# The second product of an MLP by Strassen sets, summed in DRAM

## The chip, the cores and the metric

One core of a Trainium2 chip runs the kernel. The metric is the device time of one execution in microseconds (us); for the kernel before, the median of three runs.

## What is computed

One decoder block in fp32: two gated mixers, a projection back to the residual (W_out), and an MLP with a squared ReLU (first product W1, second product W2), each behind an RMS norm. Cut to what matters here:

```python
def rmsnorm(x, g):
    return x * lax.rsqrt(jnp.mean(x * x, axis=-1, keepdims=True) + NORM_EPS) * g

def reference(x, meta_tokens, ...):                      # SEQ 512, D_MODEL 2048, D_FF 8192, 16 meta tokens
    h = concatenate([meta, x])
    u = rmsnorm(h, norm1_g)
    ...                                                  # two gated mixers, merged
    h = h + merged @ w_out
    u2 = rmsnorm(h, norm2_g)
    h = h + jnp.square(jax.nn.relu(u2 @ mlp_w1)) @ mlp_w2
    return rmsnorm(h, final_g)[:, N_META:]
```

## The kernel before

Activations lie with channels on partitions and the 512 real tokens along the free axis. Every fp32 product is made of three fp32r products: weights and activations are split into a high and a low part, and `mm3` (L609) issues high x high, high x low, low x high into one PSUM bank. A weight chunk is 128x1024 (512 KB). The class `Weights` (L34) loads it on SP's queue into a ring of four raw buffers (L78), ACT writes its high part (L102), DVE its low part (L103), into rings of four. Loads run ahead as raw buffers come free, splits two products ahead of their use.

**Stages.** The mixers and W_out run until about 1209 us. Behind the last W_out tiles (`job_WO`, L521) the residual is stored to DRAM (`h_sp`, eight pieces of 512 KB, two output tiles each), and `pre_scale` and `forms` (L546, L570) prepare W1's operands: the sums and differences of the residual that a Strassen product needs, split into high and low parts (`X`).

**W1** (L633 to L664) runs j over 32 pairs of inner tiles. Each j is one Strassen set: seven products of 8 x 3 = 24 matmuls with 256 columns each, into three banks A, B and C. The four weight blocks a, b, c, d of the set give seven weights; DVE forms four sums of them (L92) in place or in extra buffers. Results are put together from the banks with three helpers, p1, u2 and q5 (copies by ACT, sums by DVE: L641, L650, L653), scaled and clamped on DVE, squared on ACT (L662), and stored as `y_sp[j]` on POOL's queue (L663).

**W2** (L680 to L708) is a plain product: seven groups of eight inner tiles and one of four, and for each group 16 output tiles. A group's y tiles are loaded from `y_sp` on ACT's queue (L684, `yl`), split by ACT (L687, `fh`) and DVE (L688, `fl`); an output tile takes 24 matmuls of 512 columns, and DVE adds it to the accumulator `acc` (L708), which was loaded from `h_sp` at W2's start.

**The tail** (L738 to L773) does the last four inner tiles in two halves of 256 tokens, with weights kept in `keep`, and the final norm and the stores.

A scheduler sets the order of instructions on each engine from the order of the code and from the pools; within an engine they run in that order.

Of the kernel before, what the change touches and what calls it, by code (L numbers as in the profile page):

```python
# [16 lines left out]
P = 128  # L17
# [10 lines left out]
CH = 1024  # L28

# [4 lines left out]
class Weights:  # L34
# [34 lines left out]
    @staticmethod  # L69
    def _cuts(i):  # L70

        return [slice(0, CH // 2), slice(CH // 2, CH)] if i == 0 else [slice(0, CH)]

    def _load(self):
        i = self.loaded
        t = self.pool.tile([P, CH], F32, tag="raw", name=f"raw{i}", bufs=self.raw_bufs)
        for s in self._cuts(i):
            self.nc.sync.dma_start(t[:, s], self.loads[i][:, s])  # L78
        self.raw[i] = t
        self.loaded += 1  # L80
        self.live += 1

    def _split(self):
# [3 lines left out]
        for o, x, y in sums:  # L87
            if o not in self.raw:
                self.raw[o] = self.sums.tile([P, CH], F32, tag="sum", name=f"sum{o[1]}{o[0]}", bufs=3)
            while max(k for k in (x, y) if isinstance(k, int)) >= self.loaded:  # L90
                self._load()
            nc.vector.tensor_tensor(self.raw[o], self.raw[x], self.raw[y], op=ALU.add)  # L92
        while isinstance(key, int) and key >= self.loaded:
            self._load()
        raw = self.raw[key]
        if i in self.place:
            hi, lo = self.place[i]
        else:
# [15 lines left out]
    def ready(self, splits):  # L114
        while self.split < min(splits, len(self.ops)):
# [14 lines left out]
def build(ctx, tc, nc, xt_d, par_d, w_in_d, gate_d, pool_d, w_out_d, w1_d, w2_d, w2t_d, out_d):  # L130
# [46 lines left out]
    F_TILES = [8] * 7 + [4, 4]  # L177
    for f, n in enumerate(F_TILES):
        srcs = [w2_d[f * KD + m] for m in range(KD)] if n == 8 else [
            w2t_d[(f - 7) * 8 + m] for m in range(8)]  # L180
        for s in srcs:
            W.chunk(s)
# [58 lines left out]
    y_sp = [dram.tile([P, 2 * SEQ], F32, name=f"ysp{j}") for j in range(32)]  # L241
# [38 lines left out]
    with ExitStack() as mx:  # L280
# [289 lines left out]
        def pre_scale():  # L570
# [4 lines left out]
            V.tensor_scalar(s, t, 2.0 / D, EPS, op0=ALU.mult, op1=ALU.add)  # L575
# [19 lines left out]
    side.close()  # L595
    ep = xa.enter_context(tc.tile_pool(name="ep", bufs=1, side="right", reuse_waits="tile"))
    W.sums = ep
# [16 lines left out]
    if True:  # L614

        def part(name, j):
            return ep.tile([P, HS], F32, tag=name, name=f"{name}_{j}", bufs=2)

        def bank(name, j):
            return ps.tile([P, 512], F32, tag="ps", name=f"ps_{name}{j}")[:, :HS]  # L620

        def product(o, r, first):
            hi, lo = W.next()
            xh, xl = X[r]
            for k in range(8):
                s, c = slice(k * P, (k + 1) * P), slice(k * HS, (k + 1) * HS)
                mm3(o, (hi[:, s], lo[:, s]), xh[:, c], xl[:, c], first and k == 0, k == 7)
# [5 lines left out]
        for j in range(32):  # L633
            A, B, C = (bank(x, j) for x in "ABC")
            p1, u2, q5 = (part(x, j) for x in ("p1", "u2", "q5"))
            y = ep.tile([P, 2 * SEQ], F32, tag="y", name=f"y{j}", bufs=2)
            product(A, "x11", True)
            S.activation(p1, A, AF.Copy)
            W.advance()
            product(C, "x21", True)  # L640
            V.tensor_tensor(y[:, :HS], C, p1, op=ALU.add)  # L641
            W.advance()
            product(A, "t2", False)
            S.activation(u2, A, AF.Copy)
            W.advance()
            product(B, "t1", True)
            S.activation(q5, B, AF.Copy)
            W.advance()
            product(A, "t3", False)
            V.tensor_tensor(y[:, 3 * HS :], A, q5, op=ALU.add)  # L650
            W.advance()
            product(B, "x22", False)
            V.tensor_tensor(y[:, HS : 2 * HS], B, u2, op=ALU.add)  # L653
            W.advance()
            product(A, "t4", False)

            V.scalar_tensor_tensor(y[:, :SEQ], y[:, :SEQ], 0.0, rho, op0=ALU.max, op1=ALU.mult)
            V.scalar_tensor_tensor(y[:, 3 * HS :], y[:, 3 * HS :], 0.0, rho[:, HS:], op0=ALU.min,
                                   op1=ALU.mult)
            V.scalar_tensor_tensor(y[:, SEQ : 3 * HS], A, 0.0, rho[:, :HS], op0=ALU.min,  # L660
                                   op1=ALU.mult)
            S.activation(y, y, AF.Square)  # L662
            nc.gpsimd.dma_start(y_sp[j], y)  # L663
            W.advance()  # L664
    xa.close()

# [4 lines left out]


    n = len(W.ops)
    keep = [fp.tile([P, 8 * CH], F32R, name=f"keep{x}") for x in "hl"]
    for j in range(8):
        s = slice(j * CH, (j + 1) * CH)
        W.place[n - 8 + j] = (keep[0][:, s], keep[1][:, s])
    ht = fp.tile([P, KD, SEQ], F32, name="acc")
    first = 0
    for f, n in enumerate(F_TILES):  # L680
        fs = []
        for m in range(first, first + n):
            y = ftmp(f"yl{m}")
            nc.scalar.dma_start(y, y_sp[m // 2][:, (m % 2) * SEQ : (m % 2 + 1) * SEQ])  # L684
            fh = fp.tile([P, SEQ], F32R, tag="fh", name=f"fh{m}", bufs=11)
            fl = fp.tile([P, SEQ], F32R, tag="fl", name=f"fl{m}", bufs=11)
            S.activation(fh, y, AF.Copy)  # L687
            V.tensor_tensor(fl, y, fh.bitcast(F32), op=ALU.subtract)  # L688
            fs.append((fh, fl))
        if f == 0:  # L690
            for k in range(8):
                nc.scalar.dma_start(ht.rearrange("p (a k) t -> p a k t", a=2)[:, :, k, :],
                                    h_sp[k].rearrange("p (a s) -> p a s", a=2))
        first += n
        if f == len(F_TILES) - 1:
            break
        for m in range(KD):
            if n == 8 or m % 2 == 0:
                hi, lo = W.next()
            at = 0 if n == 8 else (m % 2) * n * P  # L700
            t = ps.tile([P, 512], F32, tag="ps", name=f"ps_w2_{f}_{m}")
# [107 lines left out]
```

## Time and profile before

| what | us |
|---|---|
| median of 3 runs | 2622.49 (2621.5 to 2624.58) |
| the profiled execution | 2616.56 |
| its span (first to last instruction) | 2614.8 |
| TensorE (PE) busy | 2550.6, 98% |
| VectorE (DVE) busy | 1498.0, 57% |
| ScalarE (ACT) busy | 896.7, 34% |
| GpSimd (POOL) busy | 182.9, 7% |

Busy times are of the whole span. Stages have different limits, so what counts for a stage is read in windows of it, and in what TensorE waits for there. A matmul's duration in a timeline overlaps the next one's; the distance between the starts of two is what it costs. Weight loads into TensorE (PEld) overlap matmuls.

### The profile page before, as it was taken

What the parts mean: (1) busy time and instruction counts of PE and PEld (TensorE: products, weight loads), DVE (VectorE), ACT (ScalarE), POOL (GpSimd) and SP (SyncE); (2) the same over time, 40 slices, a digit from 0 to 9 for tenths busy, and PEclk for the clock granted to TensorE, in tenths of its full rate; (3) what the DMA queues carried; (4) which work ended last, traced back from release to release, by engine and by line L of the source; (5) the groups of instructions that cost most, each with busy time, mean ns of one, the idle gap of its engine ahead of it and who ended that gap; (6) DMA issues with size and microseconds to landing.
All of it is one profiled execution on the core that took longest, in us unless ns stands there. A gap on an engine that the chain in (4) does not pass through costs nothing.

```text
span 2614.8 us, 36302 instructions
## 1 busy us (share of the span) xinstructions
PE 2550.6 (98%) x15380; PEld 2280.4 (87%) x15380; DVE 1498.0 (57%) x1759; ACT 896.7 (34%) x1096; POOL 182.9 (7%) x154
## 2 busy tenths in 40 slices
PE   8999999999999999995999999999999999999997
PEld 7888898989888898974999999999978888888887
DVE  8834574445733574449877777777644434443456
ACT  5522242223322242234444444444422222222234
POOL 2100011100211011312000000000000000000000
PEclk9999999999999999997999999999999999999999
DMA  5332223222322223231433343333463323332331
GB/s 189 97 97 89 97 73 110 93 92 86 100 94 95 91 81 105 95 119 45 134 135 127 121 138 133 133 124 121 160 215 129 129 97 129 129 129 97 125 113 65
DMA packets 91075, 296.19 MB, mean 113 GB/s; under 512 B 9760, under 2 KB 13984, under 8 KB 90912
## 3 DMA queue, kind: packets, MB, share of 16 engines
q1 hardware_dynamic: 73616, 251.82, 29.1%
q10 hardware_dynamic: 11536, 21.07, 2.4%
q0 software_dynamic: 5760, 20.97, 2.1%
q8 instruction: 120, 1.97, 0.3%
q14 instruction: 43, 0.35, 0.0%
HBM read 268.66 MB, written 25.17 MB: 112 GB/s over the span
## 4 chain that ended last, share of the span: by engine, by line
PE 91%; DVE 4%; DMA 2%; issue 1%; ACT 1%; POOL 0%; SPq 0%; ACTq 0%; DVEq 0%
PE ps_w L612 25%; PE ps_A L612 13%; PE ps_vp L332 7%; PE ps_gl L332 7%; PE ps_vl L332 7%; PE ps_gp L332 6%; PE ps_ge L332 6%; PE ps_wo L332 6%; PE ps_B L612 5%; PE ps_C L612 3%; PE ps_w2l L612 2%; PE ps_pw L332 2%; PE ga L332 2%; DMA raw<-w 1%; DVE wlo L103 1%
## 5 line engine op out<-in xcount | busy, mean ns | idle before, releaser
L102 ACT ACTIVATE whi<-raw 128x1024 fp32r<-128x1024 f32 (+1 forms) x489 | 517.6, 1059 | 1293.6 <-PE ps_w L612 434.0
L103 DVE TENSOR_TENSOR wlo<-raw,whi 128x1024 fp32r<-128x1024 f32 (+1 forms) x489 | 614.0, 1257 | 289.5 <-ACT whi L102 284.3
L612 PE MATMUL ps_w<-fh,whi 128*128 128x512 f32 x960 | 374.1, 390 | 6.6 <-ACT fh L687 6.6
L612 PE MATMUL ps_w<-fl,whi 128*128 128x512 f32 x960 | 374.1, 390 | 0.4 <-DVE fl L688 0.4
L612 PE MATMUL ps_w<-fh,wlo 128*128 128x512 f32 x960 | 373.5, 390 | 0.0
L708 DVE TENSOR_TENSOR acc<-ps_w,acc 128x512 f32<-128x512 f32 x128 | 88.5, 691 | 353.6 <-PE ps_w L612 353.6
L612 PEld LDWEIGHTS ps_w<-fh,whi 128*128 128x128 f32 x960 | 180.5, 188 | 44.9 <-ACT fh L687 7.3
L612 PEld LDWEIGHTS ps_w<-fl,whi 128*128 128x128 f32 x960 | 180.6, 188 | 39.0 <-DVE fl L688 1.5
L612 PEld LDWEIGHTS ps_w<-fh,wlo 128*128 128x128 f32 x960 | 180.6, 188 | 37.4
L332 PE MATMUL ps_vl<-uh,whi 128*128 128x264 f32 x512 | 106.0, 289 | 7.4 <-ACT whi L102 7.0
L332 PE MATMUL ps_vl<-uh,wlo 128*128 128x264 f32 x512 | 105.3, 287 | 0.0
L332 PE MATMUL ps_vl<-ul,whi 128*128 128x264 f32 x512 | 105.2, 287 | 0.0
L332 PE MATMUL ps_vp<-ul,whi 128*128 128x264 f32 x512 | 104.4, 285 | 0.0
L332 PE MATMUL ps_vp<-uh,wlo 128*128 128x264 f32 x512 | 104.3, 285 | 0.0
L332 PE MATMUL ps_vp<-uh,whi 128*128 128x264 f32 x512 | 104.2, 285 | 0.0
L332 PE MATMUL ps_gl<-ul,whi 128*128 128x512 f32 x256 | 101.2, 395 | 0.0
L332 PE MATMUL ps_gp<-ul,whi 128*128 128x512 f32 x256 | 101.2, 395 | 0.0
L332 PE MATMUL ps_ge<-ul,whi 128*128 128x512 f32 x256 | 101.2, 395 | 0.0
L332 PE MATMUL ps_gp<-uh,whi 128*128 128x512 f32 x256 | 100.7, 393 | 0.0
L332 PE MATMUL ps_ge<-uh,wlo 128*128 128x512 f32 x256 | 100.7, 393 | 0.0
L332 PE MATMUL ps_gl<-uh,wlo 128*128 128x512 f32 x256 | 100.7, 393 | 0.0
L332 PE MATMUL ps_gp<-uh,wlo 128*128 128x512 f32 x256 | 100.6, 393 | 0.0
(758 smaller groups left out, 6021.3 us busy)
## 6 DMA issues: line engine op xcount, KB each, us to landing
raw<-w SPq DMA_DIRECT2D x240, 512.0 KB, 3.6
raw<-w_in SPq DMA_DIRECT2D x159, 512.0 KB, 3.7
raw<-w_out SPq DMA_DIRECT2D x32, 512.0 KB, 3.2
ysp<-y POOLq DMA_DIRECT2D x32, 512.0 KB, 3.0
yl<-ysp ACTq DMA_DIRECT2D x64, 256.0 KB, 4.3
raw<-w2t SPq DMA_DIRECT2D x16, 512.0 KB, 3.3
ht<-xt SPq DMA_DIRECT2D x16, 264.0 KB, 6.6
raw<-gate SPq DMA_DIRECT2D x8, 512.0 KB, 3.2
```

Of the source, the lines that this page charges most:

```text
L102: nc.scalar.activation(hi[:, s], raw[:, s], AF.Copy)
L103: nc.vector.tensor_tensor(lo[:, s], raw[:, s], hi[:, s].bitcast(F32), op=ALU.subtract)
L332: PE.matmul(o, a, r, start=first and i == 0, stop=last and i == 2)
L612: PE.matmul(o, a, b, start=first and i == 0, stop=last and i == 2, skip_group_check=True)
L708: V.tensor_tensor(h, t, h, op=ALU.add)
```

## The change

W2's first 60 inner tiles (`JS` = 30 pairs) become Strassen sets as in W1. 37 steps t = 1 to 37 run; step t has the outputs p = t mod 8 (four tiles: an output pair for two halves) and sums over up to eight pairs of inner tiles, the last eight written before t. So each pair is used in eight steps in a row, the window moves on by one pair a step, and the first and last seven steps hold 1 to 7 pairs. A product of n pairs has 3n matmuls of 256 columns; its weights are n x 128 wide. A pair lies in one of nine slots (`slot`, seven forms of 256 tokens, high and low, 7 KB each on a partition), loaded on POOL's queue, split into high parts by ACT (L729) and low parts by DVE (L730). The seven forms are made in W1, where DVE computes four more (L705 to L708) into `t`; a pair is stored in two pieces. A step's result e (four quarters: DVE L742 and L746, ACT L744) is added to `h_sp` in DRAM by a DMA on POOL's queue with an accumulating write (L752). The tail's y tiles and the accumulator are loaded on POOL's queue behind the steps. In W_out, `pre_scale` stands behind the second pair of tiles, not the fourth, and one set of forms follows every second pair. The class `Weights` learns widths under 1024 and a limit for its look-ahead; the permutation `ORDER` of output channels goes along.

```diff
-    if True:
+    def strassen(name, pool, operand, put):
...
+        product(A, "x11", True)
+        S.activation(p1, A, AF.Copy)
+        W.advance()
+        product(C, "x21", True)
+        put("11", C, p1)
+        W.advance()
...
+        product(A, "t3", False)
+        put("22", A, q5)
+        W.advance()
+        product(B, "x22", False)
+        put("12", B, u2)
+        W.advance()
+        product(A, "t4", False)
+        put("21", A, None)
+        W.advance()
...
+        nc.gpsimd.dma_start(y_sp[j][:, 4 * HS :], y[:, : 3 * HS])
...
+        V.tensor_tensor(t1, x11, x12, op=ALU.subtract)
+        V.tensor_tensor(t3, x22, x12, op=ALU.subtract)
+        V.scalar_tensor_tensor(t2, x22, -1.0, t1, op0=ALU.mult, op1=ALU.subtract)
+        V.scalar_tensor_tensor(t4, t2, -1.0, x21, op0=ALU.mult, op1=ALU.subtract)
+        nc.gpsimd.dma_start(y_sp[j][:, : 4 * HS], tt)
...
+        def load_slot(j):
+            if j < JS:
+                slots[j] = sl.tile([P, 2, 7 * HS], F32R, tag="slot", name=f"slot{j}", bufs=WIN + 1)
+                nc.gpsimd.dma_start(slots[j][:, 1].bitcast(F32), y_sp[j])
+
+        def split_slot(j):
+            if j < JS:
+                hi, lo = slots[j][:, 0], slots[j][:, 1]
+                S.activation(hi, lo.bitcast(F32), AF.Copy)
+                V.tensor_tensor(lo, lo.bitcast(F32), hi.bitcast(F32), op=ALU.subtract)
+
+        for j in range(3):
+            load_slot(j)
+        split_slot(0)
+        for t, p, js in steps:
+            e = eb.tile([P, 2 * SEQ], F32, tag="e", name=f"e{t}", bufs=2)
...
+                if c == "11":
+                    split_slot(t)
+
+            strassen(f"b{t}", eb, lambda r: [tuple(slots[j][:, i, at(r)] for i in range(2)) for j in js],
+                     put)
+            nc.gpsimd.dma_start(h_sp[p], e, accum_op=ALU.add)
+            load_slot(t + 2)
...
-                    if mp_ == 3:
+                    if mp_ == 1:
                         pre_scale()
-                        forms(0)
-                        forms(2)
-                    elif mp_ > 3 and mp_ % 2 == 1:
+                    if mp_ % 2 == 1:
                         forms(mp_ - 1)
...
-            nc.scalar.dma_start(y, y_sp[m // 2][:, (m % 2) * SEQ : (m % 2 + 1) * SEQ])
...
+        nc.gpsimd.dma_start(y, y_sp[m // 2][:, c])
...
+        nc.gpsimd.dma_start(ht[:, 2 * q : 2 * q + 2, :].rearrange("p a s -> p (a s)"), h_sp[ORDER[q]])
```

The order of instructions moves at three places. The first is POOL's queue from W1's end on. Before, it ends with W1's stores; nothing else follows until the program ends:

```order
L663 DMA ysp28_134<-y28_16085 128x1024
L663 DMA ysp29_135<-y29_16313 128x1024
L663 DMA ysp30_136<-y30_16541 128x1024
L663 DMA ysp31_137<-y31_16769 128x1024
L804 UNCONDITIONAL_BRANCH
```

In the changed kernel slot loads and accumulating stores follow (names: `hsp` is the residual in DRAM, `ysp` the stored forms, `e` a step's result):

```order
L699 DMA ysp30_136<-y30_16720 128x1024
L699 DMA ysp31_137<-y31_16948 128x1024
L724 DMA slot0_17187<-ysp0_106 128x1792
L724 DMA slot1_17189<-ysp1_107 128x1792
L724 DMA slot2_17191<-ysp2_108 128x1792
L724 DMA slot3_17275<-ysp3_109 128x1792
L724 DMA slot4_17378<-ysp4_110 128x1792
L724 DMA slot5_17502<-ysp5_111 128x1792
L752 DMA hsp1_99<-e1_17195 128x1024
L724 DMA slot6_17647<-ysp6_112 128x1792
L724 DMA slot7_17813<-ysp7_113 128x1792
L724 DMA slot8_18000<-ysp8_114 128x1792
L752 DMA hsp2_100<-e2_17277 128x1024
```

The first six slot loads stand behind y31's store; those of slots 6 to 8 stand behind the first step's accumulating store.

The second place is DVE in the changed kernel's second step, which has no counterpart before (`wlo441` to `wlo445` are low parts of step 2's weights, `wlo446` is of step 3, `e2` is step 2's result, and L730 splits slots):

```order
L100 TENSOR_TENSOR raw341_17235<-raw341_17235,sum340s2_17293 128x256
L742 TENSOR_TENSOR e2_17277<-ps_Cb2_17280,p1_b2_17281 128x256
L730 TENSOR_TENSOR slot3_17275<-slot3_17275 128x1792
L112 TENSOR_TENSOR wlo441_17296<-sum340s2_17293,whi441_17295 128x256
L112 TENSOR_TENSOR wlo442_17309<-sum340s1_17291,whi442_17308 128x256
L112 TENSOR_TENSOR wlo443_17321<-raw342_17246,whi443_17320 128x256
L112 TENSOR_TENSOR wlo444_17337<-raw341_17235,whi444_17336 128x256
L730 TENSOR_TENSOR slot4_17378<-slot4_17378 128x1792
L746 SCALAR_TENSOR_TENSOR e2_17277<-ps_Ab2_17278,q5_b2_17283 128x256
L112 TENSOR_TENSOR wlo445_17350<-raw343_17256,whi445_17349 128x256
L742 TENSOR_TENSOR e2_17277<-ps_Bb2_17279,u2_b2_17282 128x256
L112 TENSOR_TENSOR wlo446_17363<-raw344_17324,whi446_17362 128x384
```

Slots 3 and 4 are split inside step 2, whose matmuls read slots 0 and 1; the last of the nine, slot 8, is split in step 3.

The third place is DVE in one full Strassen set. Before, in W1 (`wlo353` to `wlo356` and the sums are of the set's and the next set's weights, the y lines are puts):

```order
L92 TENSOR_TENSOR raw289_14128<-raw289_14128,sum288s2_14289 128x1024
L103 TENSOR_TENSOR wlo352_14351<-raw290_14160,whi352_14350 128x1024
L641 TENSOR_TENSOR y20_14261<-ps_C20_14257,p1_20_14258 128x256
L103 TENSOR_TENSOR wlo353_14385<-raw289_14128,whi353_14384 128x1024
L103 TENSOR_TENSOR wlo354_14416<-raw291_14191,whi354_14415 128x1024
L103 TENSOR_TENSOR wlo355_14447<-raw292_14354,whi355_14446 128x1024
L92 TENSOR_TENSOR sum292s1_14515<-raw294_14388,raw295_14419 128x1024
L650 TENSOR_TENSOR y20_14261<-ps_A20_14255,q5_20_14260 128x256
L103 TENSOR_TENSOR wlo356_14480<-raw293_14356,whi356_14479 128x1024
```

In the changed kernel, W1's set j = 19, with the forms of j = 18 ahead:

```order
L112 TENSOR_TENSOR wlo343_14183<-sum284s2_14180,whi343_14182 128x1024
L112 TENSOR_TENSOR wlo344_14212<-sum284s1_14178,whi344_14211 128x1024
L705 TENSOR_TENSOR t18_14140<-y18_13912 128x256
L706 TENSOR_TENSOR t18_14140<-y18_13912 128x256
L707 SCALAR_TENSOR_TENSOR t18_14140<-y18_13912,t18_14140 128x256
L112 TENSOR_TENSOR wlo345_14242<-raw286_14045,whi345_14241 128x1024
L708 SCALAR_TENSOR_TENSOR t18_14140<-t18_14140,y18_13912 128x256
L100 TENSOR_TENSOR raw285_14013<-raw285_14013,sum284s2_14180 128x1024
L686 TENSOR_TENSOR y19_14146<-ps_C19_14149,p1_19_14150 128x256
L112 TENSOR_TENSOR wlo346_14276<-raw285_14013,whi346_14275 128x1024
L112 TENSOR_TENSOR wlo347_14308<-raw287_14077,whi347_14307 128x1024
L112 TENSOR_TENSOR wlo348_14340<-raw288_14245,whi348_14339 128x1024
```

and W2's step 19, the same stretch with a slot's split ahead:

```order
L730 TENSOR_TENSOR slot19_20498<-slot19_20498 128x1792
L742 TENSOR_TENSOR e19_20729<-ps_Cb19_20732,p1_b19_20733 128x256
L112 TENSOR_TENSOR wlo562_20827<-raw410_20635,whi562_20826 128x1024
L112 TENSOR_TENSOR wlo563_20861<-raw409_20603,whi563_20860 128x1024
L112 TENSOR_TENSOR wlo564_20892<-raw411_20666,whi564_20891 128x1024
L112 TENSOR_TENSOR wlo565_20923<-raw412_20830,whi565_20922 128x1024
L100 TENSOR_TENSOR sum412s1_20990<-raw414_20864,raw415_20895 128x1024
L746 SCALAR_TENSOR_TENSOR e19_20729<-ps_Ab19_20730,q5_b19_20735 128x256
L112 TENSOR_TENSOR wlo566_20952<-raw413_20832,whi566_20951 128x1024
L100 TENSOR_TENSOR sum412s2_20992<-sum412s1_20990,raw412_20830 128x1024
```

Four operations of 256 elements (L705 to L708) come into W1's set ahead of the low parts, and one of 1792 (L730) into W2's, ahead of the put of A's first product and of the low parts.

## Rows read from the trace of the kernel before

**Rows 1.** The page: busy time by engine, then the chain's shares.

```profile
PE 2550.6 (98%) x15380; PEld 2280.4 (87%) x15380; DVE 1498.0 (57%) x1759; ACT 896.7 (34%) x1096; POOL 182.9 (7%) x154
...
PE 91%; DVE 4%; DMA 2%; issue 1%; ACT 1%; POOL 0%; SPq 0%; ACTq 0%; DVEq 0%
```

**Rows 2.** Windows: length, busy PE, PEld, DVE, ACT, POOL; PEclk, DMA, GB/s.

```profile
1500.00:1600.00 100.00, 99.82 (x829) 99.32 (x828) 73.68 (x82) 45.73 (x55) 2.65 (x5) 1.00 0.39 132
2100.00:2200.00 100.00, 100.00 (x443) 82.81 (x442) 40.16 (x46) 24.79 (x27) 0.00 (x0) 1.00 0.35 117
1900.00:1930.00 30.00, 29.16 (x126) 23.54 (x127) 14.44 (x18) 9.78 (x13) 0.00 (x0) 1.00 0.86 297
```

**Rows 3.** Timeline of TensorE: start, duration, instruction, idle before and what ended it.

```profile
1400.23 0.28 PE L612 MATMUL ps_A<-t4h,wlo 128*128 128x256 f32 x1
...
1889.16 0.28 PE L612 MATMUL ps_A<-t4l,whi 128*128 128x256 f32 x1
1889.28 0.28 PE L612 MATMUL ps_A<-t4h,wlo 128*128 128x256 f32 x1
1894.97 0.79 PE L612 MATMUL ps_w<-fh,whi 128*128 128x512 f32 x1 [5.41 <-ACT fh L687]
...
2099.65 0.39 PE L612 MATMUL ps_w<-fl,whi 128*128 128x512 f32 x1
...
2105.77 0.39 PE L612 MATMUL ps_w<-fl,whi 128*128 128x512 f32 x1
...
2552.30 0.28 PE L612 MATMUL ps_w2l<-fh,keeph 128*128 128x256 f32 x1
```

**Rows 4.** DMA landing times (W1; W2; 1885 to 1905), then POOL's last store.

```profile
raw<-w SPq DMA_DIRECT2D x98, 512.0 KB, 4.1
ysp<-y POOLq DMA_DIRECT2D x24, 512.0 KB, 3.0
...
yl<-ysp ACTq DMA_DIRECT2D x59, 256.0 KB, 4.3
...
ysp<-y POOLq DMA_DIRECT2D x1, 512.0 KB, 8.3
...
1891.78 0.53 POOL L663 DMA_DIRECT2D ysp<-y  x1 [18.64 <-ACT y L662]
```

**Rows 5.** Groups by form, DVE and ACT, 1400 to 1889 (mean ns second).

```profile
L103 DVE TENSOR_TENSOR wlo<-raw,whi 128x1024 fp32r<-128x1024 f32 x121 | 148.0, 1223 | 84.1 <-ACT whi L102 81.6
L641 DVE TENSOR_TENSOR y<-ps_C,p 128x256 f32<-128x256 f32 x24 | 10.1, 422 | 0.2 <-issue 0.2
L102 ACT ACTIVATE whi<-raw 128x1024 fp32r<-128x1024 f32 x121 | 128.4, 1061 | 157.1 <-PE ps_A L612 81.1 <-issue 37.2 <-PE ps_C L612 35.3
L644 ACT ACTIVATE u<-ps_A 128x256 f32<-128x256 f32 x24 | 8.8, 365 | 0.0
```

**Rows 6.** Windows: the first four microseconds of W2.

```profile
1895.00:1899.00 4.00, 4.00 (x9) 2.74 (x9) 1.95 (x3) 1.17 (x2) 0.00 (x0) 0.51 0.95 342
```

**Rows 7.** Timelines of DVE and TensorE, one set of W1; its fourth load.

```profile
1654.40 1.23 DVE L103 TENSOR_TENSOR wlo<-raw,whi 128x1024 fp32r<-128x1024 f32 x1 [1.65 <-ACT whi L102]
...
1660.81 1.23 DVE L92 TENSOR_TENSOR sum292s<-raw,raw 128x1024 f32<-128x1024 f32 x1 [2.31 <-DMA raw<-w]
1661.96 0.42 DVE L650 TENSOR_TENSOR y<-ps_A,q 128x256 f32<-128x256 f32 x1
...
1662.43 0.39 PE L612 MATMUL ps_A<-t4h,whi 128*128 128x256 f32 x1 [0.45 <-DVE y L650]
...
raw<-w SPq DMA_DIRECT2D x1, 512.0 KB, 5.1
```

**Rows 8.** TensorE's waits, 1200 to 1260 (total, times, longest); DVE's timeline.

```profile
PE ps_r L594 <- DVE rstd L584: 12.9, 1, 12.9
...
PE ps_wo L332 <- DVE ht L535: 5.5, 1, 5.5
...
1215.88 0.68 DVE L535 TENSOR_TENSOR ht<-ps_wo,ht 128x512 f32<-128x512 f32 x1
```

More of the change, by code (lines that the diff above doesn't have):

```diff
@@ L28 @@
 CH = 1024
+JS = 30
+WIN = 8
+ORDER = [(JS + q) % 8 for q in range(8)]
 PARAMS = ["g1", "g2", "gf", "ps", "cb", "ab", "xb", "lam", "cw0", "cw1", "cw2", "cw3"]
@@ L114, in ready @@
     def ready(self, splits):
-        while self.split < min(splits, len(self.ops)):
+        while self.split < min(splits, len(self.ops), self.limit):
             self._split()
@@ L176, in build @@
         W.strassen(*(w1_d[2 * j + n, :, h * CH : (h + 1) * CH] for n in range(2) for h in range(2)))
[L177 to L182, printed above, removed]
+    steps = []
+    for t in range(1, JS + WIN):
+        steps.append((t, t % WIN, range(max(0, t - WIN), min(t, JS))))
+    for t, p, js in steps:
+        at = slice(js[0] * P, (js[-1] + 1) * P)
+        W.strassen(*(w2_d[p + 8 * n, h, :, at] for n in range(2) for h in range(2)))
+    for q in range(8):
+        W.chunk(w2t_d[q])
     side = ctx.enter_context(ExitStack())
@@ L240, in build @@
     h_sp = [dram.tile([P, 2 * SEQ], F32, name=f"hsp{k}") for k in range(8)]
-    y_sp = [dram.tile([P, 2 * SEQ], F32, name=f"ysp{j}") for j in range(32)]
+    y_sp = [dram.tile([P, (7 if j < JS else 4) * HS], F32, name=f"ysp{j}") for j in range(32)]
     X, tok, xt = {}, {}, None
@@ L622, in product @@
         def product(o, r, first):
             hi, lo = W.next()
[L624 to L662, printed above, removed]
-            nc.gpsimd.dma_start(y_sp[j], y)
-            W.advance()
@@ L665, in build @@
-    xa.close()
+            xs = operand(r)
+            for k, (xh, xl) in enumerate(xs):
+                s = slice(k * P, (k + 1) * P)
+                mm3(o, (hi[:, s], lo[:, s]), xh, xl, first and k == 0, k == len(xs) - 1)
+        product(A, "x11", True)
[4 more added lines that the diff above has]
+        W.advance()
+        product(A, "t2", False)
+        S.activation(u2, A, AF.Copy)
+        W.advance()
+        product(B, "t1", True)
@@ L679, in build @@
[L679 to L683, printed above, removed]
-            nc.scalar.dma_start(y, y_sp[m // 2][:, (m % 2) * SEQ : (m % 2 + 1) * SEQ])
[L685 to L701, printed above, removed]
-            for k in range(n):
-                s = slice(at + k * P, at + (k + 1) * P)
-                mm3(t, (hi[:, s], lo[:, s]), fs[k][0], fs[k][1], k == 0, k == n - 1)
-            if n == 8 or m % 2 == 1:
-                W.advance()
-            h = ht[:, m, :]
-            V.tensor_tensor(h, t, h, op=ALU.add)
@@ new lines, in build @@
+        W.place[n - 4 + j] = (keep[0][:, s], keep[1][:, s])
+    W.limit = n
+    fs = []
+    for m in range(2 * JS, 64):
+        y = ftmp(f"yl{m}")
+        c = slice(0, SEQ) if m % 2 else slice(SEQ, 2 * SEQ)
+        nc.gpsimd.dma_start(y, y_sp[m // 2][:, c])
+        fh = fp.tile([P, SEQ], F32R, tag="fh", name=f"fh{m}", bufs=4)
+        fl = fp.tile([P, SEQ], F32R, tag="fl", name=f"fl{m}", bufs=4)
+        S.activation(fh, y, AF.Copy)
+        V.tensor_tensor(fl, y, fh.bitcast(F32), op=ALU.subtract)
+        fs.append((fh, fl))
```

110 lines of the change are left out of this document (86 added, 24 removed).

## The prediction

> **What bounds the kernel now.** The engine table comes first: TensorE is busy for 2550.6 of 2614.8 us [rows 1]. The chain of work that ended last says the same: nine tenths of it is TensorE [rows 1]. So a saving must come out of TensorE's own work, and everything else costs only where TensorE waits for it. Second, the table by windows. In the first MLP product (W1) TensorE is full, at full clock, and DVE busy for 74% of the time; in the second (W2) TensorE is full, DVE 40%, ACT 25% [rows 2]. W1 is what W2 is to become, so its rows price the new stage. Third, TensorE's timeline at the seams, which gives two pitches. A matmul of 256 columns follows the last one after 0.12 us (1889.28 less 1889.16); 27 of 512 columns take 6.12 us from 2099.65 to 2105.77, so 0.2267 us each. W1 ends at about 1889.4, W2's first matmul stands at 1894.97 after a wait of 5.41 us, the tail begins at 2552.30 [rows 3].
>
> **The profiled execution and the median.** It took 2616.56 us, 1.76 over its span of 2614.8; the median of the runs is 2622.49, so 5.93 us more. I sum against the profiled time and add 5.93 at the end.
>
> **Term 1, matmuls.** Before: 60 inner tiles x 16 output tiles x 3 products = 2880 matmuls of 512 columns; 2880 x 0.2267 = 652.9. After: 37 steps hold 8 x 30 = 240 pairs, each with 7 products x 3 matmuls of 256 columns: 5040 x 0.12 = 604.8. Gross gain 48.1. The real stretch from W1's end to the tail, 1889.4 to 2552.3, is 662.9: 10.0 go into the wait at its start and the low clock behind it. The tail's own 384 matmuls don't change.
>
> **Term 2, ramp-up (steps 1 to 7).** 28 pairs, 28 x 21 x 0.12 = 70.6 us of TensorE. Two things stand against that. First, slot 0 can't be loaded before W1 ends, since its memory is that of W1's operands, and on POOL's queue it stands behind the store of y31, which was issued at 1891.78, 2.4 after W1's end [rows 4]. A store of 512 KB takes 3.0 us alone and yl loads of 256 KB 4.3 [rows 4]; 896 KB I estimate at 4.2 to 5.3. So the slot lands some 7.5 us after W1's end, and its split on ACT (1792 elements; from 365 ns for 256 and 1061 for 1024 [rows 5], 1.7 us) lets TensorE start at about 9.5. Second, nine slots must be split in the first three to four steps, in the scheduler's order ahead of the weight splits there. On DVE 256 elements take 0.42 and 1024 1.22 us [rows 5], so about 0.155 + 1.04 per 1000 elements, 2.02 us for a slot. DVE's sum for steps 1 to 4: nine slots 18.2; seven weight splits and four sums a step of 128, 256, 384 and 512 elements (0.29, 0.42, 0.55, 0.69): 11 x 1.95 = 21.5; three puts a step 5.0. Together 44.7 us, against 10 x 2.52 = 25.2 of TensorE: there DVE is the bound. Start 9.5 + 44.7, then steps 5 to 7 at TensorE's pace (18 x 2.52 = 45.4): 99.6. Some 2 us of waits for loads I add, and 2 for the clock: after its wait of 5.41 us TensorE ran for some 4 us with 0.51 granted [rows 6], the 1.2 GHz level. 103.6 less 70.6 is a loss of **33**; with good overlap 22, with every wait counted twice 46.
>
> **Term 3, full steps.** Of the 23 steps with eight pairs each is built as a j of W1 is: 168 matmuls, 20.16 us. A j really took (1889.28 - 1400.23) / 24 = 20.38 [rows 3]. The difference has a place: DVE's first weight sum for the next step waits for the fourth raw load (2.31 us, at 1660.81), behind it in DVE's order stands the put of A + q5 (1661.96), and for that TensorE's seventh product waits (0.45 at 1662.43) [rows 7]. That load took 5.1 us against a median of 4.1, since three are under way at once [rows 4, 7]. In W2 the chain stays and slot work is put ahead of it. With L the time from a step's start to the slot's landing: hi 1.7, lo 2.0, put 0.4, three weight splits of 1.22 at DVE's pitch, so the third of these, which frees the buffer of that fourth load, ends at L + 7.8. TensorE paces it to about 10.9 anyhow (1655.63, in a step that began at 1644.70: 1662.43 less the wait of 0.45 and six products of 2.88; [rows 7]). So the slot costs nothing while L is under 3.1, and from there 1 us a step for each us. The slot load starts some 2 us before the step's end (its buffer is free with the third matmul of the last product, and the 21 matmuls left take 2.5); with 4.2 to 5.3 us L is 2.2 to 3.3. I take 2.7, so no stall from it, but the second and third load come 1 to 1.4 us later and so closer to the fourth: I take the 0.45 of [rows 7] in every step. 23 x 0.45 = **10** over term 1 (5 to 40).
>
> The Trainium skill ("DMA: Bandwidth & Descriptors", Anatomy of one DMA) gives for loads issued this way 2.0 us plus bytes over 436 GB/s. By that the slot would take an estimated 4.1 us, L would be 2.1, and term 3 would keep its lower value, 5, so that the total would come 5 us lower; the loads here, with company, landed later than that rule has them, 512 KB in 4.1 us in W1 [rows 4].
>
> **Term 4, ramp-down and tail.** In the last seven steps a step has 7 to 1 pairs, and the chain from a freed raw buffer over a load (4.1), two sums and a split takes longer than steps of under four pairs (10, 7.6, 5.0, 2.5 us of TensorE): about 6 us lost (4 to 12). In front of the tail, the loads of yl61 to yl63 and of the accumulator, which were issued at W2's start and hidden, stand behind the last step's store on POOL's queue; last copy, load 4.3 and split make a hole of about **6** (4 to 12).
>
> **Term 5, what moves in front.** In before, two sets of forms follow each other behind the fourth pair of W_out tiles, and DVE falls behind: TensorE waits 5.5 us for a bank and 12.9 for the norm, behind an evacuation of W_out that DVE comes to only at 1215.88 [rows 8]. With forms spread over the four pairs the first wait should go and the second shrink: **-7** (-3 to -9). What is late next there are the splits of the first summed weights behind the norm's arithmetic on DVE, which stay.
>
> **Term 6, W1.** Four more DVE operations a j (4 x 0.42 = 1.7) stand ahead of the weight split that releases the fourth load; DVE was idle for 1.65 ahead of it [rows 7], so they nearly fit. A second store of 512 KB leaves just as the loads bunch. I take 0.2 x 30 = **6** (0 to 20).
>
> **The sum.** 604.8 + 33 + 10 + 6 + 6 = 659.8 against 662.9, -3.1; with -7 and +6: **-4.1**. 2616.56 - 4.1 = 2612.5, as a median 2618.4.
>
> **Rivals.** (a) *The slot lands late, and each full step waits for it.* ACT's slot split stands ahead of the copy of p1, DVE's ahead of three weight splits. For it: the store of 512 KB that takes 3.0 us alone took 8.3 where W2 begins and the DMA engines were 86% busy [rows 2, 4]; here the slot, the accumulating store and the next step's first raw load meet. Against: W1 uses only 39% [rows 2]. It decides from L = 3.1; with 4.5, 1.4 x 22 = 31 more, 2649: slower.
>
> The Trainium skill ("Collectives: The Full Stack", The bandwidth ceiling) says an add in the DMA engines reads two sources for each write. No run here shows one; at the 297 GB/s of [rows 2] the second read of 512 KB would be an estimated 1.8 us of DMA work in each step, and if the slot waited for all of it the total would be 1.4 x 22 = 31 higher, as in (a).
>
> (b) *The ramps overlap better and the bunching doesn't show.* Ramp-up 22, full steps 5, ramp-down and tail 4 each, W1 0: 639.8 - 662.9 - 7 = -30, 2592. For it: my ramp adds DVE's work as if nothing overlapped at its start. Against: the order fixes the nine splits ahead of weights.
>
> (c) *The ramp runs at the low clock or its loads queue.* At half clock, 25 us of steps 1 to 4 become 50 beside DVE's 45 and the load's 9.5; slots 6 to 8 stand behind the first accumulating store. Some 15 more: +11, 2633. For it: TensorE starts at the low level after a long wait [rows 6]; against: there it was back after 4 us.
>
> **Chances.** The sum as forecast (2607 to 2631 on its own) 0.45; (a) 0.2; (b) 0.2; (c) 0.15. A measurement here can tell 0.2%, 5.2 us, from no change. Of the 0.45, 0.2 lie below -5.2, 0.17 within, 0.08 above. Faster: 0.2 + 0.2 = 0.40, same 0.17 and 0.03 of (c) = 0.20, slower the rest, 0.40. The range from (b) to (a), 2592 to 2648, leaves out about a tenth at each side.
>
> **What would show it.** Term 1: a pitch of 0.12 us through W2, and 5040 matmuls. Term 2: DVE full from W1's end over some 45 us, with slot splits in its timeline, and step 8 starting some 104 us after W1's end. Term 3: the period of a full step (20.6; 21.5 and a wait of TensorE for the copy of p1 or the put of A would be rival (a)), and when the slot lands in it. Term 5: no wait for a bank in W_out, the wait for the norm near 10. Term 6: a j of 20.4 to 20.6 in W1. I am wrong if a full step takes over 21 us, or if ramp-up loses under 25.

## The result, and the profile after

| | median, us | runs |
|---|---|---|
| before | 2623.84 (2619.11 to 2626.59) | 10 |
| after | 2628.90 (2623.87 to 2632.90) | 10 |

The ratio is 1.0021, with a 95% interval of 1.0012 to 1.0031: the change makes the kernel slower by 0.2%. The forecast was a gain of 4 us; it was a loss of 5. The profiled execution took 2625.76 us, 9.2 more than that of before, and its span is 2623.7. TensorE is now busy for less time than in [rows 1], and the span is longer; so the question is where TensorE waits. The page's engine line:

```profile
PE 2502.2 (95%) x17540; PEld 2333.8 (89%) x17540; DVE 1754.8 (67%) x2121; ACT 1040.2 (40%) x1353; POOL 258.2 (10%) x263
```

and the waits of TensorE over the whole span (total, times, longest):

```profile
PE ps_A L624 <- DVE y L686: 23.9, 28, 1.9
PE ps_A L624 <- ACT whi L111: 12.7, 1, 12.7
PE ps_r L606 <- DVE rstd L596: 12.1, 1, 12.1
PE ps_Ab L624 <- ACT slot L729: 10.4, 1, 10.4
PE ps_w2l L624 <- ACT fh L779: 8.9, 2, 5.3
PE ps_Ab L624 <- DVE e L746: 7.5, 12, 1.7
```

The first of these rows is new in size: in W1, which the prediction took as nearly untouched, TensorE waits 28 times for the put of A + q5. In the kernel before the profile shows 0.6 us for that between 1400 and 1889, with 0.45 of it in [rows 7].

TensorE's timeline gives the seams, as in [rows 3] (start, duration, instruction, the wait before it):

```profile
1255.39 0.28 PE L624 MATMUL ps_A<-x11h,whi 128*128 128x256 f32 x1
...
1275.18 0.28 PE L624 MATMUL ps_A<-x11h,whi 128*128 128x256 f32 x1
...
1900.02 0.28 PE L624 MATMUL ps_A<-t4h,wlo 128*128 128x256 f32 x1
1910.68 0.58 PE L624 MATMUL ps_Ab<-slot,whi 128*128 128x256 f32 x1 [10.38 <-ACT slot L729]
...
2554.96 1.53 PE L624 MATMUL ps_w2l<-fh,whi 128*128 128x256 f32 x5 [5.32 <-ACT fh L779]
...
2560.93 0.58 PE L624 MATMUL ps_w2l<-fh,whi 128*128 128x256 f32 x1 [3.61 <-ACT fh L779]
```

The first two rows are the starts of W1's j = 1 and j = 2: 19.79 us for 168 matmuls, a distance of 0.1178 us and not the 0.120 of [rows 3]. Put together with the seams of before, the stages account for the whole difference between the two profiled executions, 8.9 us of span (the medians differ by 5.1, since the profiled execution of before lies 7 us under its median and that of after 3):

| stage | before, us | after, us | difference | forecast |
|---|---|---|---|---|
| start to the norm's matmul (1221.65; 1217.27) | 1221.65 | 1217.27 | -4.4 | -7 |
| from there through W1 (to 1889.40; 1900.14) | 667.75 | 682.87 | +15.1 | +6 |
| W1's end to the tail's first matmul (2552.30; 2554.96) | 662.90 | 654.82 | -8.1 | -3.1 |
| from there to the end of the span | 62.5 | 68.7 | +6.2 | 0 |

W2 itself, its ramps and the hole before the tail included, did better than forecast. W1 and the tail lost more than that.

### The profile page after: what moved, and what is told of

It is laid out like the page before. It is cut to its first block, busy times and chain, and to the rows that moved or that the text cites. A ratio compares the mean times of both kernels' runs of the same rounds, so it can differ in the third digit from the quotient of the medians.

```text
span 2623.7 us, 41771 instructions
## 1 busy us (share of the span) xinstructions
PE 2502.2 (95%) x17540; PEld 2333.8 (89%) x17540; DVE 1754.8 (67%) x2121; ACT 1040.2 (40%) x1353; POOL 258.2 (10%) x263
## 5 line engine op out<-in xcount | busy, mean ns | idle before, releaser
L111 ACT ACTIVATE whi<-raw 128x1024 fp32r<-128x1024 f32 (+7 forms) x558 | 553.8, 1002 | 973.9 <-issue 210.5
L112 DVE TENSOR_TENSOR wlo<-raw,whi 128x1024 fp32r<-128x1024 f32 (+7 forms) x558 | 655.8, 1186 | 299.4 <-ACT whi L111 297.0
L624 PE MATMUL ps_Ab<-slot,whi 128*128 128x256 f32 x1920 | 352.0, 284 | 29.1 <-ACT slot L729 10.4
L624 PEld LDWEIGHTS ps_Ab<-slot,whi 128*128 128x128 f32 x1920 | 296.5, 190 | 36.1 <-DVE e L746 10.6
L624 PE MATMUL ps_Ab<-slot,wlo 128*128 128x256 f32 x960 | 270.9, 282 | 1.7 <-DVE wlo L112 1.7
L624 PEld LDWEIGHTS ps_Ab<-slot,wlo 128*128 128x128 f32 x960 | 183.2, 191 | 2.3 <-DVE wlo L112 2.2
L624 PE MATMUL ps_Bb<-slot,whi 128*128 128x256 f32 x960 | 175.7, 283 | 0.0
L624 PEld LDWEIGHTS ps_Bb<-slot,whi 128*128 128x128 f32 x960 | 149.6, 191 | 0.3 <-ACT whi L111 0.2
L624 PE MATMUL ps_Bb<-slot,wlo 128*128 128x256 f32 x480 | 135.6, 282 | 0.0
```

The source lines that it names most:

```text
L111: nc.scalar.activation(hi[:, s], raw[:, s], AF.Copy)
L112: nc.vector.tensor_tensor(lo[:, s], raw[:, s], hi[:, s].bitcast(F32), op=ALU.subtract)
L624: PE.matmul(o, a, b, start=first and i == 0, stop=last and i == 2, skip_group_check=True)
```

## Experiments

Times of one run, where no ratio is given, stand for themselves; what is read there is the trace. A j is the mean of the 30 distances between the starts of j = 1 to 31 in TensorE's timeline (j counts from 0); its waits for the put are summed over W1.

### The 64 bytes ahead of the operands

The change puts a tile of 64 bytes in front of W1's operands and another in front of the slots. The prediction passed over them.

```diff
-            lead = pool.tile([P, 16], F32, name="lead")
-            V.memset(lead, 0.0)
...
-        lead = sl.tile([P, 16], F32, name="lead2")
-        V.memset(lead, 0.0)
```

> The changed kernel without the two small tiles of 64 bytes that it puts ahead of W1's operands and of the slots. Theory A (where the operands begin in a partition sets the distance of two matmuls of 256 columns): the distance goes from 0.1178 back to 0.120 us in both products; W1 gets only 0 to 6 us longer, since the chain over the fourth weight load sets most of a j there, W2 some 8 us; together 5 to 15 us slower than the changed kernel. Theory B (the shorter distance comes from something else, such as the pauses): 0.1178 stays, and the time within 3 us of the changed kernel.

Measured: 2631.88 us, 1.0034 of before (1.0022 to 1.0045). The distance is back at 0.120 us, here at the starts of j = 1 and 2 (20.16 us):

```profile
1256.19 0.28 PE L622 MATMUL ps_A<-x11h,whi 128*128 128x256 f32 x1
...
1276.35 0.28 PE L622 MATMUL ps_A<-x11h,whi 128*128 128x256 f32 x1
```

Theory A holds for the distance; the time rose by 3.0 us between the medians, less than the 5 to 15 expected. And W1's j is 20.83 us with the slower matmuls, 20.86 with the faster ones: TensorE's work is not what sets it. Its waits there were 23.9 us with the 64 bytes and 12.2 without. In W2 a full step without a wait goes from 19.8 to 20.2 us, and W1's end to the tail from 654.8 to 661.2. So without the 64 bytes Strassen sets would have gained 1.7 us in W2, not 8.1.

The other way round, the kernel before with only W1's 64 bytes:

```diff
             pool = xa.enter_context(tc.tile_pool(name="xa", bufs=1, reuse_waits="tile"))
+            lead = pool.tile([P, 16], F32, name="lead")
+            V.memset(lead, 0.0)
```

> The kernel before, with only the 64 bytes ahead of W1's operands added. Theory A: W1's distance falls from 0.120 to 0.1178 us; of the 11.8 us that its 5376 matmuls save, the chain over the fourth load takes back about half: 4 to 10 us faster than before. Theory B: no change of the distance, time within 3 us of before.

Measured: 2612.94 us, 0.9962 (0.9948 to 0.9977), 9.9 us faster than before, at the far end of what was expected. A j falls from 20.33 to 20.18, and the waits for the put rise to 8.1. The two profiled executions differ by 3.7 us only, since that of before was 6 us faster than its median; where the rest of the 9.9 arises was not shown. TensorE's weight loads show the same in their durations; before:

```profile
L612 PEld LDWEIGHTS ps_C<-x21h,whi 128*128 128x128 f32 x232 | 44.5, 192 | 0.0
```

and after the change, both between 1300 and 1880:

```profile
L624 PEld LDWEIGHTS ps_B<-x22h,wlo 128*128 128x128 f32 x224 | 42.1, 188 | 0.0
```

### A fifth raw buffer

```diff
-        t = self.pool.tile([P, CH], F32, tag="raw", name=f"raw{i}", bufs=self.raw_bufs)[:, :n]
+        if self.sums is not None and i % 5 == 4:
+            t = self.sums.tile([P, CH], F32, tag="rawx", name=f"raw{i}", bufs=1)[:, :n]
+        else:
+            t = self.pool.tile([P, CH], F32, tag="raw", name=f"raw{i}", bufs=self.raw_bufs)[:, :n]
...
-                t = self.sums.tile([P, CH], F32, tag="sum", name=f"sum{o[1]}{o[0]}", bufs=3)
+                t = self.sums.tile([P, CH], F32, tag="sum", name=f"sum{o[1]}{o[0]}", bufs=2)
```

> The changed kernel with a fifth buffer for raw weight blocks from W1 on (in place of one of three for sums), so that each load starts one release earlier. Theory C (W1's 24 us of waits for the put of A + q5 are the chain freed buffer, fourth load, first sum, put): these waits fall under 5 us, a j goes from 20.86 to about 19.9, a full step of W2 from 20.25 to about 19.9; 25 to 38 us faster than the changed kernel, so 2591 to 2604. Theory D (DVE is simply behind with its four more operations a j): the waits stay over 15 us, and less than 8 us are gained.

Measured: 2613.98 us, 0.9963 (0.9951 to 0.9975), 15 us faster than the changed kernel; W1's waits 8.5 us, a j of 20.32, a full step of 20.11. Theory C has the direction and about half of the size (15 of 25 to 38 us): the chain over the fourth load carries most of the waits, but the load still lands late with a buffer that is free one release earlier.

The same edit in the kernel before, for W1's loads alone:

> The kernel before, with the fifth raw buffer in W1 alone. Theory C: a j goes from 20.33 to 20.16 on the mean, 4 to 6 us faster than before. Theory D: no change, within 2 us.

Measured: 2612.73 us, 0.9964 (0.9951 to 0.9977), a j of 20.20. More than expected by the time (10.1 us between the medians), 3.9 us by the j's of the two traces; the rest was not shown. The kernel before had this stall too, so both small edits are gains that have nothing to do with W2.

### Which of the additions to W1 costs: the store or the four operations

> The changed kernel without the 512 KB store of the four extra forms (only pair 0 stores them, and every slot is loaded from pair 0); the four DVE operations stay. Theory E (the store runs beside the bunched weight loads and delays the fourth): the waits of TensorE for the put in W1 fall from 23.9 to under 10 us, a j from 20.86 to about 20.2, as in the kernel before with the 64 bytes (20.18). Theory F (the four DVE operations delay the split that frees the fourth buffer): waits over 18 us, a j over 20.7. W2 as in the changed kernel.

```diff
-        nc.gpsimd.dma_start(y_sp[j][:, : 4 * HS], tt)
+        if j == 0:
+            nc.gpsimd.dma_start(y_sp[j][:, : 4 * HS], tt)
...
-                nc.gpsimd.dma_start(slots[j][:, 1].bitcast(F32), y_sp[j])
+                nc.gpsimd.dma_start(slots[j][:, 1].bitcast(F32), y_sp[0])
```

Measured: 2619.49 us, a j of 20.69, waits 22.7: close to theory F.

> The changed kernel without the four DVE operations that make the extra forms; the 512 KB store stays and stores the four plain quarters instead, some 2 us earlier in a j. Theory E: W1 stays at a j of 20.6 or more, waits over 15 us. Theory F: a j of about 20.2, waits under 10 us.

```diff
-        V.tensor_tensor(t1, x11, x12, op=ALU.subtract)
-        V.tensor_tensor(t3, x22, x12, op=ALU.subtract)
-        V.scalar_tensor_tensor(t2, x22, -1.0, t1, op0=ALU.mult, op1=ALU.subtract)
-        V.scalar_tensor_tensor(t4, t2, -1.0, x21, op0=ALU.mult, op1=ALU.subtract)
-        nc.gpsimd.dma_start(y_sp[j][:, : 4 * HS], tt)
+        nc.gpsimd.dma_start(y_sp[j][:, : 4 * HS], y)
```

Measured: 2596.37 us, a j of 20.00, waits 5.0. Theory F. The store of 512 KB is still there, but it leaves about 3.9 us into a j and has landed by 9.5 in every one, ahead of the fourth load; whatever else the change moved in W1 is there too. The j is below the 20.18 of the kernel before with the 64 bytes, so none of that costs anything: the loss in W1 comes with the four operations and with what leaves behind them. DVE's timeline in the changed kernel shows how 1.7 us of work come to cost. The j begins at 1545.31; the wait before an instruction stands in brackets:

```profile
1549.52 0.42 DVE L705 TENSOR_TENSOR t<-y 128x256 f32<-128x256 f32 x1
...
1550.52 1.22 DVE L112 TENSOR_TENSOR wlo<-raw,whi 128x1024 fp32r<-128x1024 f32 x1
1551.66 0.41 DVE L708 SCALAR_TENSOR_TENSOR t<-t,y 128x256 f32<-128x256 f32 x1
1551.99 1.22 DVE L100 TENSOR_TENSOR raw<-raw,sum268s 128x1024 f32<-128x1024 f32 x1
1553.13 0.41 DVE L686 TENSOR_TENSOR y<-ps_C,p 128x256 f32<-128x256 f32 x1
1554.42 2.36 DVE L112 TENSOR_TENSOR wlo<-raw,whi 128x1024 fp32r<-128x1024 f32 x2 [0.87 <-ACT whi L111]
...
1561.26 1.23 DVE L100 TENSOR_TENSOR sum272s<-raw,raw 128x1024 f32<-128x1024 f32 x1 [2.19 <-DMA raw<-w]
1562.40 0.42 DVE L686 TENSOR_TENSOR y<-ps_A,q 128x256 f32<-128x256 f32 x1
```

ACT in the same j:

```profile
1553.32 2.01 ACT L111 ACTIVATE whi<-raw 128x1024 fp32r<-128x1024 f32 x2 [3.68 <-DVE raw L100]
```

and TensorE's seventh product:

```profile
1562.15 0.28 PE L624 MATMUL ps_B<-x22h,wlo 128*128 128x256 f32 x1
1562.87 0.39 PE L624 MATMUL ps_A<-t4h,whi 128*128 128x256 f32 x1 [0.44 <-DVE y L686]
```

The seventh product starts 0.72 us after the matmul ahead of it, 0.60 over the distance, for a listed wait of 0.44: a wait costs more than its row says, so a j tells more than the sum of the waits. The sum b + s2 (L100, 1551.99) stands behind the new operations; ACT's next two splits wait 3.68 us for it (1553.32), and DVE's two low parts come in one piece (1554.42, x2). The buffers of the third and fourth load come free at 1555.6 and 1556.8, 1.2 us apart. DVE's timeline in the run without the operations, in a j that begins at 1536.82:

```profile
1541.13 1.22 DVE L100 TENSOR_TENSOR raw<-raw,sum268s 128x1024 f32<-128x1024 f32 x1
...
1543.74 1.22 DVE L112 TENSOR_TENSOR wlo<-raw,whi 128x1024 fp32r<-128x1024 f32 x1
1546.21 1.23 DVE L112 TENSOR_TENSOR wlo<-raw,whi 128x1024 fp32r<-128x1024 f32 x1 [1.25 <-ACT whi L111]
...
1552.25 1.22 DVE L100 TENSOR_TENSOR sum272s<-raw,raw 128x1024 f32<-128x1024 f32 x1 [2.09 <-DMA raw<-w]
```

There they come free 8.1 and 10.6 us into the j, 2.5 us apart.

### The operations behind that sum

```diff
-        V.tensor_tensor(t1, x11, x12, op=ALU.subtract)
...
+        def more_forms(j=j, of=of):
+            ...
+            V.tensor_tensor(t1, x11, x12, op=ALU.subtract)
...
         def put(c, x, z):
+            if c == "22" and waiting:
+                waiting.pop()()
```

> The changed kernel with the four DVE operations of a pair written out in the next j, ahead of its put of A + q5; the scheduler then sets them behind the sum b + s2, where before they stood ahead of it. Theory F1 (they cost because that sum, for which ACT's next two splits wait, stands behind them, so that the fourth buffer comes free late): a j from 20.86 to 20.0 to 20.3, waits for the put under 10 us, 15 to 25 us faster than the changed kernel. Theory F2 (DVE has too much to do in a j wherever they stand): a j over 20.6, under 8 us gained.

Measured: 2624.48 us, 1.0009 of before (0.9999 to 1.0019); a j of 20.80, waits 22.8. Theory F1 falls in its full form: the order was as wanted, the fourth buffer came free on time, and the j hardly changed. The last run took the store away too:

> The kernel with the forms behind the sum, now also without the 512 KB store of the extra forms (pair 0 alone stores them, all slots are loaded from pair 0). Left in W1 against the kernel before with the 64 bytes are then the four DVE operations, which still put off the split that frees the third load's buffer by 1.3 us (9.42 against 8.11 us into a j), while the fourth's buffer comes free on time (10.92 against 10.89). Theory L (with the fourth buffer free on time, it is the store beside the loads that makes the fourth land late): its landing comes back from 16.2 to about 15.5 us into a j, a j to 20.0 to 20.3. Theory M (third and fourth load start closer together, and that alone delays the landing): it stays at 16.0 or more, a j at 20.6 or more.

Measured: 2608.91 us, a j of 20.33, waits 13.5. One set, j = 1, takes 23.31 us there; without it a j is 20.23 and the waits are 11.7 (20.78 and 21.5 in the run above). So the j is within L's range, and the first sum, at 15.75, between L and M, nearer to L. The table sets the runs side by side: means over j = 4 to 30, in us into a j, from DVE's timeline (the end of the split that frees a buffer; the start of the sum that waits for the fourth load):

| run | third buffer free | fourth buffer free | first sum starts | wait at the put, a j |
|---|---|---|---|---|
| before, with 64 bytes | 8.11 | 10.89 | 15.54 | 0.30 |
| changed | 10.25 | 11.45 | 16.34 | 0.86 |
| changed, without the store | 10.30 | 11.48 | 16.20 | 0.81 |
| changed, without the operations | 8.11 | 10.87 | 15.47 | 0.19 |
| operations behind the sum | 9.42 | 10.92 | 16.17 | 0.76 |
| the same, without the store | 9.51 | 10.89 | 15.75 | 0.42 |

Three things put off the first sum: the fourth buffer comes free 0.56 us late, the third and fourth load start closer together, and the store runs beside them. With the buffer on time the store is worth 0.4 us and the closeness 0.2; with the buffer late the store is worth 0.14. Their shares don't add, and how the loads share the DMA engines was not taken apart further. The fourth load's own landings say the same: it was issued 10.9 us into a j in three of these runs and landed at 15.41 (before with 64 bytes), 15.66 (behind the sum, without the store) and 16.06 (behind the sum); in the changed kernel it was issued at 11.49 and landed at 16.24, with the new store issued at 7.1 and landed at 12.3.

### The tail's loads

```diff
-        nc.gpsimd.dma_start(y, y_sp[m // 2][:, c])
+        nc.sync.dma_start(y, y_sp[m // 2][:, c])
```

> The changed kernel with the tail's four y loads issued on SP's queue, not on POOL's behind the last accumulating store. Theory G (these loads are late because of what stands ahead of them on POOL's queue): the two waits of 5.3 and 3.6 us shrink to 4 together, the hole and the low clock behind it cost 4 to 6 us less; 3 to 6 us faster than the changed kernel. Theory H (all DMA engines are full there with the accumulator, weights and the y tiles, some 4.5 MB): under 2 us.

Measured: 2640.52 us, 1.0065 (1.0048 to 1.0082), 12 us slower than the changed kernel; both theories missed. The tail's first matmul waits:

```profile
2573.59 0.79 PE L624 MATMUL ps_w2l<-fh,whi 128*128 128x256 f32 x2 [20.03 <-ACT fh L779]
```

and the landings between 2540 and 2580 (the last number is the median from issue to landing) are slow on every queue:

```profile
acc<-hsp POOLq DMA_DIRECT2D x8, 512.0 KB, 14.5
raw<-w2t SPq DMA_DIRECT2D x8, 512.0 KB, 11.0
...
yl<-ysp SPq DMA_DIRECT2D x4, 256.0 KB, 12.2
```

In the new order of SP's queue six weight loads of 512 KB stand ahead of the four y loads, and the last two of them wait for buffers that splits free; ACT's order has those splits first, too. The loads were moved out of one line into a longer one, and the burst of the accumulator (4 MB) stayed beside them.

### The ramp-up

```diff
-                V.tensor_tensor(lo, lo.bitcast(F32), hi.bitcast(F32), op=ALU.subtract)
+                if not 3 <= j <= 8:
+                    V.tensor_tensor(lo, lo.bitcast(F32), hi.bitcast(F32), op=ALU.subtract)
```

> The changed kernel without the low parts of slots 3 to 8 on DVE (six of 2.02 us; these pairs are then multiplied with the unsplit values). Theory I (DVE's sum of work sets steps 1 to 4): step 8 starts 9 to 12 us earlier, 95 to 98 us after W1's end in place of 106.5. Theory K (what sets these steps are waits in turn of ACT for banks, of loads and the low clock): under 4 us earlier.

Measured: 2618.9 us. Step 8's second product starts 103.4 us after W1's end in place of 109.3: 5.9 us for 12.1 us of DVE's work. That lies between the two theories. In a window of the changed kernel over most of steps 1 to 4 DVE is busy for 35.1 of 43.3 us, TensorE for 30.4 at a clock of 0.74, between its two levels of 1.2 and 2.4 GHz:

```profile
1910.70:1954.00 43.30, 30.35 (x156) 26.98 (x157) 35.14 (x51) 25.95 (x43) 4.27 (x6) 0.74 0.73 231
```

### Both kernels repaired

> The changed kernel with the operations moved as in the run beside it, the fifth raw buffer, and the stores of the last two pairs on ACT's queue, so that slot loads on POOL's queue need not wait for them. Expected: a j of about 19.85 (waits under 4 us), the wait at W2's start from 10.4 to 3 to 6 us, a full step of 19.95; 28 to 38 us faster than the changed kernel, 2591 to 2601. If W1's waits had another cause, 2610 or more.

```diff
-            nc.gpsimd.dma_start(y_sp[j], y)
+            nc.scalar.dma_start(y_sp[j], y)
             continue
```

Measured: 2608.61 us, 0.9951 (0.9938 to 0.9964), 20 us faster than the changed kernel and not the 28 to 38 expected, close to the 2610 that was to speak for another cause of W1's waits. W2's first wait is 3.7 us and step 8 comes 6.7 us sooner after W1's end, as meant. POOL's queue issues slot 0's load 16.5 us ahead of W1's end (1889.92), and TensorE starts 3.9 us behind it:

```profile
1873.42 0.55 POOL L732 DMA_DIRECT2D slot<-ysp  x1 [17.03 <-DVE y L698]
...
1893.78 0.58 PE L627 MATMUL ps_Ab<-slot,whi 128*128 128x256 f32 x1 [3.70 <-ACT slot L737]
```

A full step stays at 20.20, and a j at 20.39, with 10.4 us of waits, since the fourth load still lands late (the first sum starts 0.66 us later than in the run below).

The kernel before with W1's 64 bytes and its fifth buffer, the two edits shown above:

> The kernel before with both small edits, the 64 bytes and the fifth raw buffer in W1. Expected, if the chain of the fourth load was all that kept the shorter distance from showing: a j of 19.8, 18 to 21 us faster than before, 2602 to 2606. Against the run beside it this says what Strassen sets in W2 are worth when W1's waits are gone: by the terms 5 to 10 us.

Measured: 2603.72 us, 0.9933 (0.9920 to 0.9946): as expected, faster than both kernels, and 4.9 us below the repaired Strassen version, where a gain of 5 to 10 us from Strassen sets was expected. By stage, repaired against repaired: W2 648.7 against 663.9 us, W1's j 20.39 against 19.91 (15 us over W1), the tail to its last matmul 57.2 against 48.6. So Strassen sets gain 15 us in W2, and W1 and the tail lose 15 and 8.6.

## Why the prediction was wrong

**The step that failed is term 6, W1.** It took DVE's 1.65 us of idle time ahead of one split [rows 7] as room for four operations of 0.42 us, and put them and their store at 0.2 us a j. Measured: +15.1 us from the norm to W1's end for the forecast +6, and a j of 20.86 for 20.33, past the 20.4 to 20.6 that was to bear the term out. Without the four operations, the store kept but leaving earlier, a j is 20.00. They stand ahead of the sum b + s2, for which ACT's next two splits wait; the third load's buffer comes free 2.1 us later than in the kernel before with the 64 bytes and the fourth's 0.56, and the store that follows the operations runs beside these two loads. The fourth load was already the last to arrive, so the first sum starts 0.80 us later and a j takes 0.68 us more. The place ahead of that sum is not the whole reason: behind it, with the fourth buffer free on time, a j was still 20.80, and 20.33 without the store. How late release, closeness of the loads and the store share the rest stays open.

**Term 1 left an edit out.** I read the change for what it computes and did not cost the two tiles of 64 bytes. They shorten each matmul of W1 and of the steps by 0.0022 us: 5040 x 0.1178 = 593.7 in place of 604.8, of which W2's stretch shows 6.4 us (654.8 for 661.2). In W1 the 11.8 us that 5376 x 0.0022 make don't show in the changed kernel: from the norm to its end it took 682.9 us with the tiles and 682.3 without. The gain in W2 kept the loss at 0.2%; without the tiles the loss is 0.34%.

**Term 2, ramp-up, was near.** TensorE started 10.5 us after W1's end (forecast 9.5), and step 8 began 106.5 after it (103.6): its second product stands at 2009.43, less 24 x 0.1178, against 1900.14. The loss is 37.2 over 28 x 21 x 0.1178 = 69.3; forecast 33. But its reason, DVE's sum of work, is half right: of 12.1 us taken off DVE, 5.9 came back. And of its two reasons for the late start one is wrong: slot 0's memory does not hold its load back until W1 ends, since with the last stores on ACT's queue the load was issued 16.5 us ahead of W1's end (the fifth buffer alone left the wait at 10.5 us). The order of POOL's queue alone kept it behind y31's store.

**Term 3, full steps, was right in its sum, in part by luck.** The second products of steps 8 and 31 begin here:

```profile
2009.43 0.28 PE L624 MATMUL ps_Cb<-slot,whi 128*128 128x256 f32 x1
...
2474.77 0.40 PE L624 MATMUL ps_Cb<-slot,whi 128*128 128x256 f32 x2
```

Step 31's first product is three matmuls shorter, so 23 steps take 2474.77 - 2009.43 + 3 x 0.1178 = 465.69 us, 20.25 each, 0.46 over 168 x 0.1178; forecast 0.45. The wait for the put of A is there, but in 11 of the 23 steps and not in each, up to 1.71 us. And at the distance of 0.120 that the prediction used, in the run without the 64 bytes, a full step is 20.39, only 0.23 over its matmuls. Its reason for the slow load of [rows 7], three loads under way at once, is not in the trace: when that load was issued at 1655.65, one other was under way (1652.78 to 1657.78). The slot's split starts 2.7 to 4.5 us into a step, 3.2 on the mean (forecast 2.7, limit 3.1). Where it is late, rival (a) shows, in three steps of 21; in one of them, which begins at 2026.45, ACT splits the slot late:

```profile
2030.84 1.70 ACT L729 ACTIVATE slot<-slot 128x1792 fp32r<-128x1792 f32 x1 [2.71 <-DMA slot<-ysp]
```

and TensorE waits for the copy of p1 behind it:

```profile
2032.86 0.51 PE L624 MATMUL ps_Ab<-slot,whi 128*128 128x256 f32 x2 [0.60 <-ACT p_b L648]
```

So (a) named a mechanism that is there and cost little. The median landings over the full steps (issue to landing, last number):

```profile
raw<-w SPq DMA_DIRECT2D x87, 512.0 KB, 4.4
slot<-ysp POOLq DMA_DIRECT2D x21, 896.0 KB, 4.9
hsp<-e POOLq DMA_DIRECT2D x23, 512.0 KB, 6.6
```

The slot takes 4.9 us, within the 4.2 to 5.3 taken from rows. The Trainium skill ("DMA: Bandwidth & Descriptors", Anatomy of one DMA) gives an estimated 4.1 by its fit; with other transfers under way the trace is 0.8 above it. The accumulating store takes 6.6 us against 3.0 for a plain one of its size in [rows 4], and 5.2 for the plain store of the new forms in W1, beside two weight loads. That it is slower agrees in direction with the two reads for each write that the Trainium skill ("Collectives: The Full Stack", The bandwidth ceiling) states, though the company differs, and no run here separates the two.

**Term 4.** Ramp-down and the hole before the tail cost 13.4 us together (2472.3 to 2554.96, less 69.3; forecast 12). The hole goes on behind the tail's first matmuls, a second wait of 3.61 us and a granted clock of 0.75 from 2554.96 to 2575 (1.00 in the tail before), and that part, 6.2 us, was not in the sum: the four y loads land one by one, at 2551.4 and from 2560.2 to 2562.9, beside 4 MB of accumulator.

**Term 5.** -4.4 for -7: the wait for a bank shrank from 5.5 [rows 8] to 2.5, and the wait for the norm stayed at 12.1. Over all traces the gain is smaller: the norm's matmul starts at 1219.1 on the mean of the ten kernels with the new order of W_out, and at 1222.0 on that of the four without.

**The balance.** Against the forecast of -4.1 the profiled span came out at +8.9: term 6 is worth 9.1 of the 13, the tail 6.2, term 5 2.6, and W2 gave 5.0 back. Neither of the two signs of being wrong showed: a full step stayed under 21 us and the ramp-up lost more than 25.

## What to carry to other kernels

Idle time on an engine ahead of one instruction is not room for new work: follow what stands between the new work and the next release on every engine, since a split on a second engine may wait for something far behind it in the first one's order. Where a stage is bound by a chain of release, load and use, a faster matmul only lengthens the wait; give the chain a buffer first. And cost every line of a diff, the ones that compute nothing too: here W2's stretch got 8.1 us shorter with two tiles of 64 bytes, and 1.7 without them.

## What the runs showed of the hardware that was not expected

- A tile of 64 bytes ahead of the operands changes the distance of two matmuls of 256 columns: 0.120 us without it, 0.1178 with it, and a weight load takes 192 or 188 ns. It was taken out of the one kernel and put into the other. Why an offset of 64 bytes does this was not shown; the tail's matmuls stay at 0.120 in the kernels before and after.
- A load that starts close behind another lands later. With the fourth buffer free at the same time (10.9 us into a j), that load landed at 15.4 us when the third was 2.8 us ahead, at 15.7 when it was 1.4 ahead, and at 16.1 with a store of 512 KB beside them; the sum that waits for it started at 15.5, 15.75 and 16.2.
